# Gated delta mixer: a group's blocks are made and stored with its projections, and only their inversion stays in the next iteration

## The chip, the cores and the metric

The kernel runs on one core of one Trainium2 chip. The metric is the device time of one execution in microseconds (us); lower is better. Engine names: PE is TensorE, DVE is VectorE, ACT is ScalarE, POOL is GpSimd, SP is SyncE, which only issues DMAs here. Each engine works through its own instructions in the order in which they stand in the program.

## The reference

The program is a four-layer encoder trunk on 256 tokens of width 1024; each layer has a token mixer and a SwiGLU channel mixer. The change touches the mixer of layer 1, a bidirectional gated delta rule. It has 8 query and key heads, each serving 2 value heads of width 128. One direction of it, cut to what matters:

```python
decay = _exp_segsum(g_cs)                       # exp(g_i - g_j) for j <= i, else 0
a_mat = jnp.where(strict, jnp.einsum('bnhid,bnhjd->bnhij', k_beta, k) * decay, 0.0)
rhs = jnp.concatenate([v_beta, k_beta * jnp.exp(g_cs)[..., None]], axis=-1)
sol = lax.linalg.triangular_solve(a_mat, rhs, left_side=True, lower=True, unit_diagonal=True)
qk = jnp.einsum('bnhid,bnhjd->bnhij', q, k) * decay
...
o = rms_norm(o_fwd + o_bwd, norm_w) * jax.nn.silu(z.astype(f32).reshape(bt, L, GDN_V_HEADS, GDN_HEAD_DIM))
```

So for each head and direction a unit triangular matrix, made of key products and decays, has to be inverted or solved with.

## The kernel before, in words

The mixer (`gdn`, L554 to L842) works on 8 groups, one per query and key head; a group is 2 value heads, in two directions. The 256 tokens are taken as two blocks of 128. Four generators make the stages of a group `a`:

- `into(a)` (L609): projections of query and key (`pqk`) and of value (`pv`) on PE, a convolution and SiLU on DVE and ACT, norms, the masked products `km` of key with key (`kk`) and of query with key (`qkm`), and the values turned to token order (`vtok`).
- `base(a)` (L660): for each of the 2 heads `decay_exps` (L396): two matmuls into the PSUM bank `bc`, four ACT ops (L408) and one Exp (L409) give the decays `e`; POOL makes `off` (L669), DVE four diagonal blocks `u` (L672), POOL `e` times `qkm` (L676). POOL then stores the 8 blocks `u` to HBM (`gat`, L681) and loads the 64 inner blocks of 16 by 16 (`yr`, L688). ACT copies them (L689, L690), 28 POOL ops in 14 steps invert all 64 (L696, L698), ACT copies them back (L702, L703), and they go through HBM (`inv`, L705) to `dg` (L707).
- `levels(a)` (L710): POOL spreads `dg` and `u` (`lx` L717, `lb` L721), PE projects `z` (`pz`), and three rounds of small matmuls (`pst`, `pw`, `px`) with copies between them build the inverses of the 128 by 128 blocks (`ls`: L746, L771).
- `apply(a)` (L775): matmuls `pu` and `po`, a norm (`ysq` on ACT, `oms` on DVE, `omr` on POOL L820, `yo` on DVE), transposes `yt`, gating, the split `yh`, `yl`, and the output projection's first half (`first`, into `acc_o`). `yh` and `yl` of groups 0 to 6 also go to HBM (`spill`, L833). The second half of the output projection (`second`, PSUM `proj`) comes in the last three iterations and loads them back (`again`, L598: `ych`, `ycl`).

Iteration `a` of the loop at L839 weaves `apply(a-3)`, `levels(a-2)`, `base(a-1)` and `into(a)`, and from a = 8 on `second`. This is only the order in which the program is written. A scheduler of the tile framework then places the instructions of each engine by its own model of time and by the free buffers, and that order is fixed on the chip. PSUM has one bank `base`, shared by `bc` and `pz`, and one bank `side`, shared by `ss`, `pk` and `vp`. The buffers that the change bears on are `km` (4, also used by `ych` and `ycl`), `off` (7), `e` (8) and `u` (3).

Of the kernel before, what the change touches and what calls it, by code (L numbers as in the profile page):

```python
# [7 lines left out]
F32 = mybir.dt.float32  # L8
F32R = mybir.dt.float32r
# [3 lines left out]
P = 128  # L13
L = 256
# [28 lines left out]
class Trunk:  # L43
# [510 lines left out]
    def gdn(self, i):  # L554
        nc, t, j = self.nc, self.t, 0
        wk = self.mx
# [37 lines left out]
        st = {}  # L594
# [3 lines left out]
        def again(a):  # L598
            if a == 7:
                return ys[a]  # L600
            y = [wk.tile([P, 2, L], F32R, name=n, tag="km", bufs=4) for n in ("ych", "ycl")]
            for c in range(2):
                nc.sync.dma_start(y[c].bitcast(F32), spill[a, c])
            return y
# [4 lines left out]
        def into(a):  # L609
            pq = self.project(t["gdn_w"][a, 0], name="pqk")  # L610
            yield
            qk = wk.tile([P, 2, L], F32, name="qk", tag="qk", bufs=1)
            for m in range(2):
                self.conv_silu(pq, m, cw[:, a, m], qk[:, m])
                yield
            sq = wk.tile([P, 2, L], F32, name="qsq", tag="qsq", bufs=1)
            nc.scalar.square(sq, qk)
            pv = self.project(t["gdn_w"][a, 1], name="pv")
            yield

            ss = side[0].tile([P, 2, 2], F32, name="ss", tag=side[1])
            for m in range(2):
                for s in range(2):
                    nc.tensor.matmul(ss[:, m, s:s + 1], sq[:, m, s * P:(s + 1) * P], self.ones[:, 0:1], start=True, stop=True)
            qe, ke, kr, kn = (wk.tile([P, 2], F32, name=n, tag=n, bufs=b) for n, b in (("qe", 5), ("ke", 2), ("kr", 2), ("kn", 2)))
            nc.vector.tensor_scalar(out=ke, in0=ss[:, 1], scalar1=EPS, scalar2=None, op0=ALU.add)
            nc.vector.tensor_scalar(out=qe, in0=ss[:, 0], scalar1=EPS, scalar2=EPS * P, op0=ALU.add, op1=ALU.mult)
            nc.gpsimd.tensor_tensor(out=kn, in0=ke, in1=self.half.to_broadcast([P, 2]), op=ALU.pow)
            nc.vector.reciprocal(out=kr, in_=ke)
            nk = wk.tile([P, 2, 2, 2], F32, name="nk", tag="nk", bufs=5)  # L630
            nc.vector.tensor_tensor(out=nk, in0=nb.rearrange("p s (d h) -> p s d h", d=2)[:, :, :, 2 * a:2 * a + 2],
                                    in1=kr.unsqueeze(2).unsqueeze(3).to_broadcast([P, 2, 2, 2]), op=ALU.mult)
            yield
            vt = wk.tile([P, 2, L], F32, name="vt", tag="vt", bufs=1)
            for m in range(2):
                self.conv_silu(pv, m, cw[:, a, 2 + m], vt[:, m])
                yield
            pair = []
            for m, mask in ((1, strict), (0, self.incl)):
                pk = side[0].tile([P, 2, L], F32, name="pk", tag=side[1])  # L640
                for s in range(2):
                    nc.tensor.matmul(pk[:, s], qk[:, 1, s * P:(s + 1) * P], qk[:, m], start=True, stop=True)
                km = wk.tile([P, 768], F32, name="km", tag="km", bufs=4)
                self.masked(km, pk, mask)
                pair.append(km)
                yield
            kk, qkm = pair
            vs = []
            for m in range(2):
                vp = side[0].tile([P, 2, P], F32, name="vp", tag=side[1])  # L650
                for s in range(2):
                    nc.tensor.transpose(vp[:, s], vt[:, m, s * P:(s + 1) * P], self.ident)
                v = wk.tile([P, 2, P], F32, name="vtok", tag="vtok", bufs=8)
                for s in range(2):
                    nc.scalar.activation(v[:, s], vp[:, s], AF.Copy, scale=kn[:, s:s + 1])
                vs.append(v)
                yield
            st[a] = kk, qkm, vs, nk, qe

        def base(a):  # L660
            kk, qkm, vs, nk, qe = st[a]
            u = wk.tile([P, 8, P], F32, name="u", tag="u", bufs=3)
            es, offs = [], []
            for m in range(2):
                h = 2 * a + m
                e = self.decay_exps(pos, row, h, 32 + h, 8, bank)
                yield
                off = wk.tile([P, 2, P], F32, name="off", tag="off", bufs=7)
                nc.gpsimd.tensor_tensor(out=off.rearrange("p a b -> p (a b)"), in0=e[:, 128:384], in1=kk[:, 128:384],  # L669
                                        op=ALU.mult)  # L670
                for o, s, d in blocks:
                    nc.vector.scalar_tensor_tensor(out=u[:, 4 * d + 2 * m + s], in0=e[:, o:o + P],  # L672
                                                   scalar=nk[:, s, d, m:m + 1], in1=kk[:, o:o + P],
                                                   op0=ALU.mult, op1=ALU.mult)
                yield
                nc.gpsimd.tensor_tensor(out=e, in0=e, in1=qkm, op=ALU.mult)  # L676
                es.append(e)
                offs.append(off)
                yield
            gat = self.dr.tile([64, 2064], F32, name=f"gat{a}")  # L680
            nc.gpsimd.dma_start(gat.rearrange("(u b) x -> u (b x)", b=8)[:, :P * P].rearrange("u (p c) -> p u c", c=P), u)  # L681
            yield

            yb = lambda n: wk.tile([64, 16, 16], F32, name=n, tag=n, bufs=1)
            yr, y = yb("yr"), yb("yb")
            fl = lambda v, p: v[p].rearrange("p r c -> p (r c)")
            fw, bw = slice(0, 32), slice(32, 64)
            nc.gpsimd.dma_start(yr, gat[:, :16 * P].rearrange("q (r c) -> q r c", c=P)[:, :, :16])  # L688
            nc.scalar.copy(fl(y, fw), fl(yr, fw))  # L689
            nc.scalar.copy(fl(y, bw), fl(yr, bw)[:, ::-1])  # L690
            yield
            for k in range(1, 15):
                sh = [64, k, 15 - k]
                tm = wk.tile([64, 64], F32, name="ybt", tag="ybt", bufs=2)[:, :k * (15 - k)].rearrange(
                    "p (r c) -> p r c", r=k)
                nc.gpsimd.tensor_tensor(out=tm, in0=y[:, :k, k:k + 1].to_broadcast(sh),  # L696
                                        in1=y[:, k:k + 1, k + 1:].to_broadcast(sh), op=ALU.mult)
                nc.gpsimd.tensor_tensor(out=y[:, :k, k + 1:], in0=y[:, :k, k + 1:], in1=tm, op=ALU.add)  # L698
                yield
            nc.gpsimd.memset(y.rearrange("p r c -> p (r c)")[:, ::17], 1.0)  # L700
            yo = yb("yr")
            nc.scalar.copy(fl(yo, fw), fl(y, fw))  # L702
            nc.scalar.copy(fl(yo, bw), fl(y, bw)[:, ::-1])  # L703
            inv = self.dr.tile([8, 8, 16, 16], F32, name=f"inv{a}")
            nc.gpsimd.dma_start(inv.rearrange("u b r c -> (u b) r c"), yo)  # L705
            dg = wk.tile([P, 8, 16], F32, name="dg", tag="dg", bufs=2)
            nc.gpsimd.dma_start(dg, inv.rearrange("u b r c -> (b r) u c"))  # L707
            st[a] = es, vs, offs, u, dg, nk, qe
# [66 lines left out]
        def apply(a):  # L775
# [58 lines left out]
            if a > 0:  # L834
                first(a - 1)

        first, second, close = self.halves(t["gdn_wo"], ys.get, again)
        run = lambda f, a: [f(a)] if 0 <= a < 8 else []
        for a in range(11):  # L839
            weave(*run(apply, a - 3), *run(levels, a - 2), *run(base, a - 1), *run(into, a),  # L840
                  *([second(*((0, 1, 2), (3, 4), (5, 6))[a - 8])] if a > 7 else []))
# [530 lines left out]
```

## Time and profile before

| | |
|---|---|
| runs (3): median, lowest, highest | 2034.78 us, 2032.54 us, 2035.58 us |
| the profiled execution: its time, its span | 2029.43 us, 2027.7 us |
| mean granted TensorE clock | 0.932 |
| PE, DVE, ACT, POOL busy, share of the span | 88%, 71%, 52%, 17% |

The profile is of one execution, and its times are counted from the start of its span. The gated delta mixer lies at about 525 to 940 us. Its loop over the groups begins with the first `pqk`, and the last output projection of the mixer ends at about 938 us. A busy share is an average over stages with different limits; the prediction reads the stretch of this mixer alone. A row of the timeline has the start, the duration, the engine, the line, the operation with output and inputs, and in brackets the idle time of the engine before it and what ended that.

### The profile page before, as it was taken

How to read it: one execution, taken by the hardware profiler on the slowest of the kernel's cores; microseconds unless marked ns; L12 is line 12 of the kernel's file. 1: busy time of each engine (PE TensorE's matmuls, PEld its weight loads, DVE VectorE, ACT ScalarE, POOL GpSimd, SP SyncE). 2: the span in 40 equal slices, each digit the busy share in tenths (PEclk: the TensorE clock that was granted, in tenths of full speed). 3: DMA queues.
4: the chain of work that ended last, by engine and by line, in shares of the span. 5: the costliest groups of instructions: out<-in, count | busy, mean ns of one | idle time of the engine just before them, and what ended most of it. 6: DMA issues, size and time to landing. Idle time of an engine off the chain costs nothing.

```text
span 2027.7 us, 35637 instructions
## 1 busy us (share of the span) xinstructions
PE 1782.4 (88%) x13948; PEld 1526.6 (75%) x13948; DVE 1441.8 (71%) x2542; ACT 1044.9 (52%) x1888; POOL 353.7 (17%) x536
## 2 busy tenths in 40 slices
PE   5999969999599988975999976969997999978998
PEld 5899848888588877763878765658886899857886
DVE  5999957997788676434989458456646999946653
ACT  4777746553466556423545334444434677734442
POOL 1121110000167465621000002010001111110000
PEclk9999979999799999986999966979998999988999
DMA  6344335776344343612767587256644334416652
GB/s 230 118 134 146 115 105 163 243 223 210 120 138 133 99 122 101 182 46 102 236 201 238 175 302 194 68 198 186 187 152 163 125 130 141 127 52 202 185 185 93
DMA packets 105848, 317.66 MB, mean 157 GB/s; under 512 B 11036, under 2 KB 35180, under 8 KB 103632
## 3 DMA queue, kind: packets, MB, share of 16 engines
q1 hardware_dynamic: 99472, 296.03, 45.6%
q0 software_dynamic: 5920, 18.83, 3.1%
q8 instruction: 109, 1.79, 0.4%
q14 instruction: 59, 0.48, 0.1%
q10 hardware_dynamic: 288, 0.52, 0.1%
HBM read 287.49 MB, written 27.85 MB: 156 GB/s over the span
## 4 chain that ended last, share of the span: by engine, by line
PE 71%; DVE 11%; POOL 5%; ACT 5%; issue 4%; DMA 3%; SPq 0%; DVEq 0%; POOLq 0%; ACTq 0%
PE proj L87 10%; PE proj L88 10%; PE proj L89 10%; PE acc_o L87 5%; PE acc_o L88 5%; PE acc_o L89 5%; PE proj L94 5%; PE proj L95 4%; PE proj L96 4%; DVE wlo L80 3%; PE yp L525 2%; POOL ybt L696 2%; ACT whi L79 2%; POOL yb L698 1%; DMA s_w<-wt 1%
## 5 line engine op out<-in xcount | busy, mean ns | idle before, releaser
L80 DVE TENSOR_TENSOR wlo<-raw,whi 128x1024 fp32r<-128x1024 f32 x475 | 599.3, 1267 | 242.2 <-ACT whi L79 235.3
L79 ACT CAST whi<-raw 128x1024 fp32r<-128x1024 f32 x475 | 495.0, 1049 | 413.5 <-PE proj L88 180.8
L87 PE MATMUL proj<-whi,xh 128*128 128x512 f32 x768 | 307.7, 403 | 23.9 <-DVE xl L192 20.0
L89 PE MATMUL proj<-wlo,xh 128*128 128x512 f32 x768 | 304.2, 396 | 0.0
L88 PE MATMUL proj<-whi,xl 128*128 128x512 f32 x768 | 304.2, 396 | 0.0
L94 PE MATMUL proj<-xh,whi 128*128 128x256 f32 x792 | 232.7, 295 | 9.2 <-DVE acc L421 5.0
L96 PE MATMUL proj<-xh,wlo 128*128 128x256 f32 x792 | 229.4, 290 | 0.0
L95 PE MATMUL proj<-xl,whi 128*128 128x256 f32 x792 | 227.3, 287 | 0.0
L87 PEld LDWEIGHTS proj<-whi,xh 128*128 128x128 f32 x768 | 147.2, 192 | 57.5 <-DVE xl L192 21.6
L87 PE MATMUL acc_o<-whi,yh 128*128 128x512 f32 x448 | 179.6, 404 | 5.8 <-ACT yh L191 5.8
L218 POOL TENSOR_TENSOR rs<-ms,mhalf 128x1 f32<-128x1 f32 x32 | 20.9, 653 | 935.0 <-DVE ms L217 930.8
L88 PE MATMUL acc_o<-whi,yl 128*128 128x512 f32 x448 | 179.2, 400 | 0.0
L89 PE MATMUL acc_o<-wlo,yh 128*128 128x512 f32 x448 | 176.3, 396 | 0.0
L89 PEld LDWEIGHTS proj<-wlo,xh 128*128 128x128 f32 x768 | 146.8, 191 | 31.4 <-issue 0.2
L88 PEld LDWEIGHTS proj<-whi,xl 128*128 128x128 f32 x768 | 147.2, 192 | 30.9 <-issue 0.7
L94 PEld LDWEIGHTS proj<-xh,whi 128*128 128x128 f32 x792 | 155.0, 196 | 15.6 <-DVE acc L421 5.8
L95 PEld LDWEIGHTS proj<-xl,whi 128*128 128x128 f32 x792 | 155.3, 196 | 0.1
L96 PEld LDWEIGHTS proj<-xh,wlo 128*128 128x128 f32 x792 | 155.0, 196 | 0.3
L408 ACT ACTIVATE e<-bc,csn 128x256 f32<-128x256 f32 (+1 forms) x320 | 108.7, 430 | 39.0 <-PE bc L403 39.0
L255 PE MATMUL ht<-ident,xn 128*128 128x128 f32 x128 | 29.2, 381 | 108.8 <-DVE xn L287 48.1
L421 DVE SCALAR_TENSOR_TENSOR acc<-proj,cw,acc 128x255 f32<-128x255 f32 (+1 forms) x256 | 118.3, 476 | 2.0
L500 POOL TENSOR_TENSOR e<-e,cbm 128x768 f32<-128x768 f32 x32 | 60.7, 1897 | 324.1 <-DVE cbm L852 130.7
(357 smaller groups left out, 3416.8 us busy)
## 6 DMA issues: line engine op xcount, KB each, us to landing
raw<-w_gu SPq DMA_DIRECT2D x176, 512.0 KB, 4.5
raw<-ssd_w SPq DMA_DIRECT2D x96, 512.0 KB, 3.8
raw<-w_dn SPq DMA_DIRECT2D x88, 512.0 KB, 3.6
raw<-gdn_w SPq DMA_DIRECT2D x48, 512.0 KB, 4.2
raw<-ssd_wo SPq DMA_DIRECT2D x32, 512.0 KB, 3.5
nwb<-norm_w POOLq DMA_DIRECT2D x16, 512.0 KB, 5.1
s_w<-wt SPq DMA_DIRECT2D x16, 512.0 KB, 5.4
s_cl<-clb SPq DMA_DIRECT2D x16, 512.0 KB, 5.2
```

What stands on the lines that cost most here:

```text
L79: nc.scalar.copy(hi, raw)
L80: nc.vector.tensor_tensor(out=lo, in0=raw, in1=hi.bitcast(F32), op=ALU.subtract)
L87: nc.tensor.matmul(out, x[0], w[0], start=first, stop=False, **kw)
L88: nc.tensor.matmul(out, x[1], w[0], start=False, stop=False, **kw)
L89: nc.tensor.matmul(out, x[0], w[1], start=False, stop=last, **kw)
L94: nc.tensor.matmul(out, hi, x[0], start=first, stop=False, **kw)
L95: nc.tensor.matmul(out, hi, x[1], start=False, stop=False, **kw)
L96: nc.tensor.matmul(out, lo, x[0], start=False, stop=last, **kw)
L408: nc.scalar.activation(e[:, o], src, AF.Relu, scale=-1.0, bias=n)
L421: nc.vector.scalar_tensor_tensor(out=acc[:, a:b], in0=ps[:, m, a + o:b + o], scalar=cw[:, k:k + 1], in1=acc[:, a:b], op0=ALU.mult, op1=ALU ...
L500: (nc.gpsimd if hl % 2 == 0 else nc.vector).tensor_tensor(out=es[hl], in0=es[hl], in1=cbm, op=ALU.mult)
L525: nc.tensor.matmul(yp[64 * hh:64 * hh + 64, m, a:b], xdt[:, s, d, 2 * m + hh], es[2 * m + hh][:, o:o + b - a], start=(n == 0), stop=(n == 3))
```

## The change

The second half of `into(a)` now also makes the decays, `off`, `u`, `e` times `qkm` and the store `gat` of group `a`; `base(a)`, an iteration later, begins with the load `yr`. In iteration `a` these instructions are now written for group `a`, where they were for group `a-1`. `km` gets 3 buffers where it had 4, `off` 8 where it had 7. The number of instructions and their operands stay the same. Lines behind the edit move down by at most 3.

```diff
-            y = [wk.tile([P, 2, L], F32R, name=n, tag="km", bufs=4) for n in ("ych", "ycl")]
+            y = [wk.tile([P, 2, L], F32R, name=n, tag="km", bufs=3) for n in ("ych", "ycl")]
...
-                km = wk.tile([P, 768], F32, name="km", tag="km", bufs=4)
+                km = wk.tile([P, 768], F32, name="km", tag="km", bufs=3)
...
-            st[a] = kk, qkm, vs, nk, qe
-
-        def base(a):
-            kk, qkm, vs, nk, qe = st[a]
+
             u = wk.tile([P, 8, P], F32, name="u", tag="u", bufs=3)
             es, offs = [], []
             for m in range(2):
                 h = 2 * a + m
                 e = self.decay_exps(pos, row, h, 32 + h, 8, bank)
                 yield
-                off = wk.tile([P, 2, P], F32, name="off", tag="off", bufs=7)
+                off = wk.tile([P, 2, P], F32, name="off", tag="off", bufs=8)
                 nc.gpsimd.tensor_tensor(out=off.rearrange("p a b -> p (a b)"), in0=e[:, 128:384], in1=kk[:, 128:384],
                                         op=ALU.mult)
...
             nc.gpsimd.dma_start(gat.rearrange("(u b) x -> u (b x)", b=8)[:, :P * P].rearrange("u (p c) -> p u c", c=P), u)
-            yield
+            st[a] = es, vs, offs, u, nk, qe, gat
+
+        def base(a):
+            es, vs, offs, u, nk, qe, gat = st[a]
 
             yb = lambda n: wk.tile([64, 16, 16], F32, name=n, tag=n, bufs=1)
```

How the scheduler's order moves is shown at three places; numbers behind a tile's name are those of its buffer.

**POOL, around the store of group 6.** Before; ahead of these rows stand the 28 ops of group 5's inversion and `omr` of `apply(3)`, and `off_9826` and `e_9722` belong to group 7:

```order
L707 DMA dg_9045<-inv5_9043 128x8x16
L833 DMA spill_5411<-yh_8772 128x512
L717 TENSOR_TENSOR lx_9060<-dg_9045,lev_5319 128x256
L833 DMA spill_5411<-yl_8773 128x512
L669 TENSOR_TENSOR off_9484<-e_9347,km_8941 128x256
L676 TENSOR_TENSOR e_9347<-e_9347,km_8962 128x768
L681 DMA gat6_9553<-u_9067 128x8x128
L721 TENSOR_TENSOR lb_9712<-u_9067,lev_5319 32x256 x4
L669 TENSOR_TENSOR off_9826<-e_9722,km_9592 128x256
L688 DMA yr_9584<-gat6_9553 64x16x16
L676 TENSOR_TENSOR e_9722<-e_9722,km_9613 128x768
```

Now; ahead stand the 28 ops of group 5's inversion with `omr` of `apply(2)` among them:

```order
L833 DMA spill_5411<-yl_8145 128x512
L717 TENSOR_TENSOR lx_9095<-dg_9071,lev_5319 128x256
L628 TENSOR_TENSOR kn_9518<-ke_9516,half_69 128x2
L666 TENSOR_TENSOR off_9043<-e_9034,km_8962 128x256
L673 TENSOR_TENSOR e_9034<-e_9034,km_8983 128x768
L666 TENSOR_TENSOR off_9073<-e_9059,km_8962 128x256
L673 TENSOR_TENSOR e_9059<-e_9059,km_8983 128x768
L678 DMA gat6_9080<-u_9030 128x8x128
L721 TENSOR_TENSOR lb_9747<-u_9030,lev_5319 32x256 x4
L688 DMA yr_9102<-gat6_9080 64x16x16
```

Both products of both heads of a group now stand ahead of its store, where before the first head's stood behind the store of the group before. Counted against `apply`, the store is one group ahead: before, group 5's inversion stands next to `omr` of `apply(3)`, now group 6's does. `omr` itself stands behind 28, 20, 28, 28 and 20 of the 28 inversion ops for `apply(0)` to `apply(4)` before, and behind 7, 18, 17, 16 and 17 now.

**PE, the `bc` matmuls of group 1**, between the value projection of group 1 (`pv`) and `pz` of group 0; `vp` are transposes of group 0's values. Before:

```order
L96 MATMUL pv_5731<-xh_72,wlo_5728 128x256
L403 MATMUL bc_5910<-csr_5402,sel_82 128x256 x2
L652 MATMUL vp_5601<-ident_63,vt_5570 128x128 x2
L94 MATMUL pz_5992<-xh_72,whi_5982 128x256
L95 MATMUL pz_5992<-xl_73,whi_5982 128x256
L96 MATMUL pz_5992<-xh_72,wlo_5983 128x256
```

Now:

```order
L96 MATMUL pv_5754<-xh_72,wlo_5751 128x256
L403 MATMUL bc_5886<-csr_5402,sel_82 128x256 x2
L652 MATMUL vp_5601<-ident_63,vt_5570 128x128 x2
L403 MATMUL bc_5911<-csr_5402,sel_82 128x256 x2
L652 MATMUL vp_5607<-ident_63,vt_5570 128x128 x2
L94 MATMUL pz_6022<-xh_72,whi_6012 128x256
```

The second head's `bc`, which stood an iteration later and amid a projection, now follows the first with one pair of transposes between them, and `pz`, in the same PSUM bank, follows with another pair. Group 2 has its two `bc` pairs likewise; from group 3 on a projection or other work lies between the two.

**SP, the loads of the tail.** `ych` and `ycl` of groups 0 to 2, between weight loads (`raw`). Before:

```order
L603 DMA ych_9736<-spill_5411 128x512
L603 DMA ycl_9737<-spill_5411 128x512
L603 DMA ych_9838<-spill_5411 128x512
L603 DMA ycl_9839<-spill_5411 128x512
L76 DMA raw_10273<-gdn_w 128x1024
L76 DMA raw_10279<-gdn_w 128x1024
L76 DMA raw_10334<-gdn_wo 128x1024
L603 DMA ych_9912<-spill_5411 128x512
L603 DMA ycl_9913<-spill_5411 128x512
```

Now:

```order
L603 DMA ycl_9767<-spill_5411 128x512
L603 DMA ych_9865<-spill_5411 128x512
L603 DMA ycl_9866<-spill_5411 128x512
L603 DMA ych_9941<-spill_5411 128x512
L76 DMA raw_10273<-gdn_w 128x1024
L76 DMA raw_10279<-gdn_w 128x1024
L76 DMA raw_10334<-gdn_wo 128x1024
L603 DMA ycl_9942<-spill_5411 128x512
L603 DMA ych_10244<-spill_5411 128x512
```

Before, a group's two loads stand together; `ych_9736` is group 0's. Now group 0's `ych` stands four rows earlier, and group 2's `ycl` (`ycl_9942`) stands behind three weight loads. With 3 buffers a group's `ycl` takes the buffer that the `ych` of the group before had.

## Rows read from the trace of the kernel before

**Rows 1.** Busy time by windows: PE, PEld, DVE, ACT, POOL, clock, DMA share, GB/s.

```profile
560.00:600.00 40.00, 35.01 (x258) 33.62 (x257) 37.32 (x73) 26.70 (x53) 28.62 (x46) 0.93 0.51 160
...
760.00:800.00 40.00, 34.03 (x541) 29.87 (x540) 28.07 (x56) 22.46 (x54) 25.10 (x45) 0.94 0.31 98
```

**Rows 2.** The chain that ended last, 676 to 880 us, by line.

```profile
by line: POOL ybt L696 11.2%; POOL yb L698 9.7%; issue 9.1%; DMA yr<-gat 6.2%; POOL lb L721 5.6%; ACT whi L79 3.5%; PE acc_o L87 3.5%; ACT e L408 3.2%; PE acc_o L88 2.7%; POOL e L676 2.2%; POOL omr L820 2.0%; PE acc_o L89 1.9%; PE px L768 1
```

**Rows 3.** Waits of PE, 560 to 840 us: total, times, longest.

```profile
PE pst L756 <- DVE ls L746: 4.8, 2, 3.9
PE yt L827 <- DVE yo L822: 4.5, 3, 1.9
PE pst L756 <- ACT ls L771: 3.3, 3, 2.4
PE pz L94 <- ACT e L408: 3.0, 3, 1.2
```

**Rows 4.** Timeline of PE, three places early in the loop.

```profile
551.19 0.79 PE L403 MATMUL bc<-csr,sel 128*128 128x256 f32 x2 [2.38 <-ACT e L408]
...
594.02 0.59 PE L652 MATMUL vp<-ident,vt 128*128 128x128 f32 x2 [2.36 <-DVE km L852]
595.61 0.58 PE L94 MATMUL pz<-xh,whi 128*128 128x256 f32 x1 [1.00 <-ACT e L408]
```

**Rows 5.** Timeline of ACT in the tail.

```profile
858.46 0.40 ACT L689 COPY yb<-yr 32x256 f32<-32x256 f32 x1 [2.76 <-DMA yr<-gat]
...
859.30 1.04 ACT L79 CAST whi<-raw 128x1024 fp32r<-128x1024 f32 x1
...
869.59 0.40 ACT L702 COPY yr<-yb 32x256 f32<-32x256 f32 x1 [5.04 <-POOL yb L698]
...
870.43 0.60 ACT L815 ACTIVATE ysq<-po 128x512 f32<-128x512 f32 x1
870.93 0.26 ACT L764 COPY sw<-pw 128x128 f32<-128x128 f32 x1
```

**Rows 6.** Timeline of DVE in the tail.

```profile
855.73 1.23 DVE L80 TENSOR_TENSOR wlo<-raw,whi 128x1024 fp32r<-128x1024 f32 x1 [1.16 <-ACT whi L79]
860.38 1.23 DVE L80 TENSOR_TENSOR wlo<-raw,whi 128x1024 fp32r<-128x1024 f32 x1 [3.42 <-ACT whi L79]
...
861.78 1.70 DVE L746 TENSOR_TENSOR ls<-lx,px 32x256 f32<-32x256 f32 x4
```

**Rows 7.** Timeline of PE in the tail.

```profile
831.70 0.65 PE L827 MATMUL yt<-ident,yo 128*128 128x128 f32 x4 [1.92 <-DVE yo L822]
...
858.75 0.69 PE L744 MATMUL px<-lx,lw 32*32 32x32 f32 x56
863.63 0.61 PE L756 MATMUL pst<-ident,ls 32*32 32x32 f32 x32 [4.19 <-DVE ls L746]
...
868.47 0.47 PE L762 MATMUL pw<-sT,u 32*32 32x32 f32 x32
871.24 0.47 PE L768 MATMUL px<-ls,sw 32*32 32x32 f32 x32 [2.30 <-ACT sw L764]
```

**Rows 8.** DMA issues: KB each, median us from issue to landing.

```profile
ycl<-spill SPq DMA_DIRECT2D x7, 256.0 KB, 2.9
```

**Rows 9.** Waits of POOL, 560 to 945 us.

```profile
POOL off L669 <- ACT e L409: 23.8, 5, 8.1
```

**Rows 10.** Timeline of POOL: the second head of group 5, its store, the first product of group 6.

```profile
769.34 0.74 POOL L669 TENSOR_TENSOR off<-e,km 128x256 f32<-128x256 f32 x1 [8.07 <-ACT e L409]
...
779.52 0.86 POOL L688 DMA_DIRECT2D yr<-gat  x1
780.39 1.82 POOL L676 TENSOR_TENSOR e<-e,km 128x768 f32<-128x768 f32 x1
```

**Rows 11.** Instructions on tile u: duration in ns, min/median/max, first and last start.

```profile
L672 DVE SCALAR_TENSOR_TENSOR u<-e,nk,km x64: 339/351/1322, 564.7 to 846.3; 128x128 f32<-128x128 f32 x64
```

**Rows 12.** Instructions on tile ybt, in the same form.

```profile
L696 POOL TENSOR_TENSOR ybt<-yb x112: 205/270/1357, 580.4 to 869.1; 64x14 f32<-64x14 f32 x16, 64x26 f32<-64x26 f32 x16, 64x36 f32<-64x36 f32 x16, 64x44 f32<-64x44 f32 x16
```

## The prediction, as it was made before the run

> **What bounds the kernel now.** The change touches one mixer, so I read that mixer's stretch and not the page's shares of the whole span. First the busy time by windows [rows 1]: in the middle of the loop over the groups PE is busy for 34.03 of 40 us, and no other engine for more than 28.07. At its start DVE is the fullest, with 37.32 of 40. So the loop is bound by PE with some idle time, except at its start, where an idle PE is partly the shadow of a full DVE. Next the chain that ended last [rows 2]: from 676 to 880 us it lies for 37% (11.2, 9.7, 6.2, 5.6, 2.2 and 2.0) on the inversion's POOL ops, the load `yr`, `lb`, `e` and `omr`. So POOL is tied into the chain although PE has the work. What that costs PE is in PE's waits [rows 3]: 4.8 us for `ls` from DVE, 4.5 for `yo`, which waits for `omr`, 3.3 for `ls` from ACT, 3.0 for the decays that hold the bank of `pz`. These 15.6 us are most of what a better order inside the loop can win. The tail's waits [rows 7] are read below. The chain alone would promise far more than the waits allow: while the chain runs through POOL, PE mostly has other work.
>
> **The change, part by part.** Nothing is removed or added. Per group these move one iteration earlier: two `bc` pairs on PE, two times five ops on ACT, eight `u` on DVE, two `off` and two `e` products and one store on POOL. Their sum is the same, so only places and buffers can change the time. Outside this mixer every engine's order stays the same.
>
> 1. **The tail, a gain.** Before, the inversion of group 7 runs at 858 to 870 us, when few groups are left, and its ACT copies stand in ACT's queue ahead of things PE needs. Now that inversion lies one group earlier and these copies stand before the last projection's work. First place: ACT waits 2.76 us for `yr` [rows 5], the weight conversion behind it begins only at 859.30, DVE's subtraction at 860.38 and the four `ls` adds at 861.78 [rows 6], and PE waits 4.19 us [rows 7]. Without the copies the subtraction follows the one that ended at 856.96, and the adds can start when `px` ends at 859.44; they take 1.70, so PE goes on at about 861.3 in place of 863.63: 2.3 us. Second place: ACT waits 5.04 us for the inversion's end [rows 5], with `ysq` and `sw` behind it, and PE's `px` waits 2.30 [rows 7]. `po` is through at 868.47; `sw` comes 0.5 behind `ysq` and `px` 0.3 behind `sw`, so 869.3 in place of 871.24: 1.9 us. Together **-4.2**. What is late next there is the chain `ysq`, `oms`, `omr`, `yo`, `yt`, which moves up with them.
>
> 2. **The loads of the tail, a loss.** With 3 buffers, a group's `ycl` can be loaded only when the group before it has left PE; a load takes 2.9 us to land [rows 8]. Groups 1 and 2, and 2 and 3, stand close together on PE. Between 1 and 2 only short `px` work and two matmuls lie, some 1.2 us, so 1.7 us are open; but PE already idles 1.92 us there for `yt` [rows 7], and that wait falls into the same gap, which leaves 0.5. Between 2 and 3 `yt` (0.65) and some 1 us of small matmuls lie: 1.2 open. SP's queue holds the next weights behind a waiting load, but they are for later groups. Taken: **+1.7**. Bounds: 0, and 5.8 if both loads are fully bare.
>
> 3. **The two `bc` pairs side by side, a loss at the start.** The second needs the first's bank. At 551.19 such a second pair waited 2.38 us [rows 4]; one pair of transposes (0.59) now lies between, which leaves 1.8, for groups 1 and 2, and `pz` of group 0 waits 1.8 in place of about 1.0 [rows 3]: 4.4 in all. DVE is 93% busy there [rows 1], so I take half: **+2.2** (bounds 0 and 4.4). From group 3 on a projection covers the first head's decays; without that cover each group would pay 2.4.
>
> 4. **Waits that go at the start.** `vp` of group 1 waited 2.36 us for `km` through the bank `side`, and `pz` 1.00 [rows 4]; in the new order a value projection lies ahead of that `vp`, and `pz` comes earlier. 3.4, and half for the same reason: **-1.7** (bounds 0 and -3.4).
>
> 5. **`omr` earlier in POOL's queue.** It stands behind 16 to 18 inversion ops instead of 20 or 28. PE's three waits for `yo` inside the loop's full part sum to 4.5 us [rows 3], the tail's 1.92 is in term 2. Where it stood behind all 28, the wait should go (1.1); where behind 20, three ops of some 0.3 us [rows 12] go. Taken: **-1.8** (bounds 0 and -4.5).
>
> 6. **DVE's order near `ls`.** In DVE's new order the adds of `levels(4)` stand ahead of a weight subtraction (1.23 [rows 6]) and one SiLU product instead of behind them, but behind two mask products more. PE waited up to 3.9 us for them [rows 3]. Taken: **-1.0** (bounds 0 and -3.9).
>
> 7. **The store later on POOL.** Both heads' decays and the first `e` product now stand ahead of the store; before, the next group's first product (1.82) ran in the shadow of the `yr` load [rows 10]. POOL waited 23.8 us in five times for decays ahead of `off` [rows 9], 4.8 a time, and I take it that this slack covers the 1.82: **0**. If it does not, 1.82 for each of groups 3 to 7: 9.1.
>
> 8. **The rings.** `e` now has all 8 buffers in flight. The decays of group a+4 wait for `po` of group a, and PE's order has that `po` ahead of the `bc`: nothing. `u` keeps 3 and is free when `levels` of three groups back has ended, just ahead of the new `bc`: nothing.
>
> Sum: -4.2 + 1.7 + 2.2 - 1.7 - 1.8 - 1.0 = **-4.8 us**. The profiled execution took 2029.43, so its like would take 2024.6. The median of the runs is 2034.78, 5.35 above that execution; on its scale the forecast is **2030.0 us**. What a measurement here can tell from no change is about 0.2%, 4.1 us; the forecast lies just beyond that.
>
> **A rule against it.** Of 64 `u` products of one shape half take under 351 ns and the longest 1322 [rows 11]; the small POOL products run from 205 to 1357 [rows 12]. The Trainium skill, page "SBUF — State Buffer", section "Who interferes with whom", says that a DVE instruction with two SBUF inputs and a POOL instruction that reads SBUF take turns: the first has the shared ports for its whole length. By that rule, with which these spreads agree, the second head's `u` now meet the first head's `e` product ahead of every store.
>
> **The rivals.**
>
> *Slower: the store sets the pace.* Each store now waits for a second head's decays (about 2.4 us, the wait at 551.19 [rows 4]) and an `e` product (1.82). The slack is 4.8 a time [rows 9]; a `u` product held up once costs a further 1.0 (1322 less 351 ns [rows 11]), which makes 5.2 and is more than the slack. So this decides from the point where the decays come that late. Against it: the 8.07 us wait [rows 10]. Price: 9.1 for five groups, and the 1.8 of term 5 is lost because the inversion starts later: -4.8 + 9.1 + 1.8 = +6.1, 2040.9 us; with a held-up `u` in each of the five, 2045.8.
>
> *No change: the loads eat the tail's gain.* Both loads bare (5.8 for 1.7): -0.7, 2034.1 us. For it: SP's strict queue. Against it: the `yt` gap.
>
> *A larger gain: the slots follow the chain.* If the 37% of the chain [rows 2] is a true cycle (store, load, inversion, `omr`, `yt`, next decays), the group ahead breaks it, and PE's 15.6 us of waits [rows 3] go: -15.6 - 4.2 + 1.7 = -18.1, 2016.7 us. Against it: PE's waits change hands when an order is new, and seldom all go.
>
> *The scheduler keeps the old places.* The order shows the inversion one group ahead from group 3 on, so there is little for it: 2034.8.
>
> **How the numbers follow.** Forecast 0.43, slower rival 0.24, no change 0.18, larger gain 0.12, old places 0.03. The forecast lies near the border, and its unknown terms spread it by several us: of its 0.43 I count 0.34 as faster and 0.09 as within 0.2%. Faster: 0.34 + 0.12 = 0.46. Same: 0.09 + 0.17 + 0.03 = 0.29. Slower: 0.24, and 0.01 of the no-change case: 0.25. The range takes in all of the forecast's bounds, the slower rival nearly to its end and most of the larger gain: 2018 to 2045.
>
> **What would show it.** Right: the wait of 4.19 at the last but one `levels` falls to about 2 and ACT has no `yr` copy between 850 and 880 us of the old scale; `omr` follows `oms` within 1 us; two new waits of PE for decays appear near 570 and 595 us; PE waits for `ycl` once or twice near 830 us. Wrong: `off` on POOL no longer waits for decays but for POOL itself, PE's waits for `yo` grow, and the first output matmuls of successive groups (`acc_o`) come further apart than before. Then term 7 was not free.

## The result, and the profile after

The changed kernel takes 2048.05 us (median of 4 runs), the kernel before 2034.03 us beside it: a ratio of 1.0069, 95% interval 1.0052 to 1.0087. It is **slower by 14 us**, where the prediction had it faster by 4.8. The profiled execution after has a span of 2047.7 us.

First the whole stretch, from the first decay matmul to the first matmul behind the mixer's last sum: PE's busy time, then PEld, DVE, ACT, POOL, the granted clock, the DMA share. Before:

```profile
548.00:939.50 391.50, 336.64 (x4545) 299.12 (x4545) 243.61 (x490) 198.29 (x443) 205.81 (x367) 0.92 0.35 107
```

After:

```profile
550.70:957.80 407.10, 345.60 (x4544) 305.79 (x4544) 247.14 (x490) 199.09 (x443) 213.97 (x367) 0.89 0.33 102
```

The stretch is 15.6 us longer. The two profiled executions differ by more than the medians do (spans of 2027.7 and 2047.7 us, 20.0 apart against 14.0), since that of the kernel before was a short one; the other 4.4 us lie outside the stretch. The same matmuls keep PE busy for 9.0 us more, with a granted clock of 0.89 in place of 0.92, and PE is idle for 6.6 us more (61.5 against 54.9). More than half of these 15.6 us is thus PE working more slowly, and no term of the prediction has that.

Where it happens: I gave every PE instruction a weight (the lower fifth of the spacing of its kind over the profiles), summed from the first decays, and looked how much later than in the kernel before the same sum is reached. This **lag** is a working figure from one execution each, and lags of a few us say nothing by themselves: a kernel that is level in time with the kernel before (e8 below) has 3.6 at 921 us. After the change it is 6.1 us at 576 us of the old scale, 13.8 at 639, and from there it stays between 10 and 21, with 17.1 at 921. So the loss is made while the loop fills, in two steps, and is not won back. The windows of the two steps, before:

```profile
568.00:578.00 10.00, 8.37 (x69) 7.96 (x68) 9.61 (x19) 8.21 (x19) 8.70 (x8) 1.00 0.60 165
578.00:588.00 10.00, 10.00 (x83) 9.89 (x82) 8.72 (x17) 7.76 (x15) 6.66 (x17) 1.00 0.51 166
588.00:598.00 10.00, 6.64 (x41) 5.97 (x40) 10.00 (x22) 6.18 (x13) 8.90 (x18) 0.81 0.53 176
598.00:608.00 10.00, 10.00 (x75) 10.00 (x75) 7.72 (x15) 4.58 (x10) 6.23 (x9) 0.85 0.26 86
```

And after, 3 us later on the scale:

```profile
571.00:581.00 10.00, 5.59 (x29) 4.75 (x28) 8.61 (x19) 9.06 (x23) 8.45 (x7) 0.78 0.60 166
581.00:591.00 10.00, 10.00 (x74) 9.90 (x74) 4.00 (x11) 3.70 (x7) 7.20 (x21) 0.88 0.02 3
591.00:601.00 10.00, 9.59 (x78) 9.29 (x76) 9.96 (x19) 4.70 (x8) 9.16 (x16) 1.00 0.60 193
601.00:611.00 10.00, 4.20 (x18) 3.67 (x19) 9.11 (x14) 8.21 (x22) 6.81 (x6) 0.64 0.53 180
```

PE begins 199 matmuls in these 40 us where it began 268. DVE and ACT are not fuller but emptier (31.7 against 36.0 us, 25.7 against 26.7): nobody is overloaded, everybody waits for somebody. What PE waits for, in PE's timeline after; the brackets hold the idle time before a row:

```profile
571.23 0.39 PE L403 MATMUL bc<-csr,sel 128*128 128x256 f32 x2
572.53 0.41 PE L652 MATMUL vp<-ident,vt 128*128 128x128 f32 x2 [0.91 <-DVE km L852]
573.67 0.50 PE L403 MATMUL bc<-csr,sel 128*128 128x256 f32 x2 [0.73 <-ACT e L408]
575.40 0.44 PE L652 MATMUL vp<-ident,vt 128*128 128x128 f32 x2 [1.23 <-ACT vtok L655]
577.38 0.58 PE L94 MATMUL pz<-xh,whi 128*128 128x256 f32 x1 [1.54 <-ACT e L408]
...
605.78 0.80 PE L403 MATMUL bc<-csr,sel 128*128 128x256 f32 x2 [4.17 <-ACT e L408]
608.03 0.58 PE L94 MATMUL pqk<-xh,whi 128*128 128x256 f32 x1 [1.45 <-DVE acc L421]
```

At the first step PE thus idles 4.4 us in four waits. Before, the same place had two, of 1.6 us together:

```profile
569.73 0.41 PE L652 MATMUL vp<-ident,vt 128*128 128x128 f32 x2 [0.90 <-DVE km L852]
570.87 0.39 PE L94 MATMUL pz<-xh,whi 128*128 128x256 f32 x1 [0.73 <-ACT e L408]
```

The two waits that are new are 1.54 us of `pz` for the bank `base` and 1.23 us of the second transposes for `vtok`, which empties the bank `side`.

And before, the second pair of group 1 came one projection later, at no wait at all:

```profile
584.31 0.28 PE L403 MATMUL bc<-csr,sel 128*128 128x256 f32 x1
585.10 0.47 PE L403 MATMUL bc<-csr,sel 128*128 128x256 f32 x1
```

At the second step the decays themselves are late. ACT works in order, and ahead of them stand two weight casts that wait for their loads:

```profile
599.55 1.05 ACT L79 CAST whi<-raw 128x1024 fp32r<-128x1024 f32 x1 [3.60 <-DMA raw<-gdn_w]
...
602.97 1.05 ACT L79 CAST whi<-raw 128x1024 fp32r<-128x1024 f32 x1 [1.09 <-DMA raw<-gdn_w]
...
604.38 1.35 ACT L408 ACTIVATE e<-bc,csn 128x256 f32<-128x256 f32 x4
```

The first pair's matmul ended at 600.6 and was read from 604.38 on. That ACT keeps its order is also in the Trainium skill, page "PSUM — Partial Sum Buffer", section "Engine vs sequencer instructions": the queues of ScalarE, VectorE and GpSimd are strict FIFO. The trace agrees: the decays were read 3.8 us after their matmul, behind the casts, and PE's next pair waited 4.17 us. DMA had stood nearly still (share 0.02) at 581 to 591. I take that to be why the loads are late: PE had left `pz` after 18 of its 48 matmuls for `pqk`, so that the weights of both stayed in use.

What did the earlier decays buy there? The store of group 1, before and after:

```profile
592.37 0.96 POOL L681 DMA_DIRECT2D gat<-u  x1 [0.24 <-issue]
```

```profile
595.41 0.96 POOL L678 DMA_DIRECT2D gat<-u  x1
```

That is 44.4 and 44.7 us behind the first decays: nothing. Before, the scheduler had already put group 1's decays early enough for that store, one pair beside each projection.

PE's waits after, 560 to 850 us, the lines that answer to [rows 3] and the new ones:

```profile
PE pst L756 <- ACT ls L771: 6.1, 2, 4.9
PE bc L403 <- ACT e L408: 5.4, 3, 4.2
PE vp L652 <- DVE km L852: 4.8, 4, 2.1
PE proj L88 <- DMA ycl<-spill: 2.4, 1, 2.4
PE pz L94 <- ACT e L408: 2.0, 2, 1.5
PE yt L827 <- DVE yo L822: 1.9, 2, 1.0
```

The tail, which answers to [rows 7]:

```profile
838.06 0.51 PE L88 MATMUL proj<-whi,ycl 128*128 128x512 f32 x1 [2.38 <-DMA ycl<-spill]
...
885.86 0.47 PE L756 MATMUL pst<-ident,ls 32*32 32x32 f32 x32 [2.60 <-DVE ls L746]
...
891.67 0.47 PE L768 MATMUL px<-ls,sw 32*32 32x32 f32 x32 [0.44 <-ACT sw L764]
```

### The profile page after: what moved, and what is told of

It is laid out like the page before. It is cut to its first block, busy times and chain, and to the rows that moved or that the text cites. A ratio compares the mean times of both kernels' runs of the same rounds, so it can differ in the third digit from the quotient of the medians.

```text
span 2047.7 us, 35626 instructions
## 1 busy us (share of the span) xinstructions
PE 1794.5 (88%) x13948; PEld 1536.6 (75%) x13948; DVE 1445.7 (71%) x2542; ACT 1048.6 (51%) x1888; POOL 361.3 (18%) x536
## 4 chain that ended last, share of the span: by engine, by line
PE 68%; DVE 13%; DMA 5%; POOL 5%; ACT 4%; issue 4%; SPq 0%; DVEq 0%; POOLq 0%; ACTq 0%
PE proj L87 10%; PE proj L88 9%; PE proj L89 9%; PE acc_o L87 5%; PE acc_o L88 5%; PE acc_o L89 4%; PE proj L94 4%; PE proj L95 4%; PE proj L96 4%; DVE wlo L80 3%; PE yp L525 2%; DVE acc L421 1%; ACT whi L79 1%; POOL ybt L696 1%; POOL yb L698 1%
## 5 line engine op out<-in xcount | busy, mean ns | idle before, releaser
L88 PEld LDWEIGHTS proj<-whi,xl 128*128 128x128 f32 x768 | 148.0, 193 | 31.3 <-issue 0.7
L94 PEld LDWEIGHTS proj<-xh,whi 128*128 128x128 f32 x792 | 155.5, 197 | 15.6 <-DVE acc L421 5.8
```

Source lines behind the costliest of these rows:

```text
L88: nc.tensor.matmul(out, x[1], w[0], start=False, stop=False, **kw)
L94: nc.tensor.matmul(out, hi, x[0], start=first, stop=False, **kw)
```

## The experiments

All times are ratios to the kernel before, run beside each kernel, with the 95% interval; the lag is at 576, 639 and 921 us of the old scale. The execution that gives a lag is not always a typical one: executions of e10 spread over 12 us and its profiled one is the longest (2046.70 us, median 2038.76), as are those of e9 and e15; those of e1 and e14 are the shortest (2037.81 and 2040.95 us, medians 2044.95 and 2046.21).

| kernel | ratio | lag, us |
|---|---|---|
| the change | 1.0069 (1.0052 to 1.0087) | 6.1, 13.8, 17.1 |
| e1 groups 0 to 3 moved | 1.0046 (1.0031 to 1.0061) | 6.1, 13.7, 10.9 |
| e2 groups 4 to 7 moved | 1.0002 (0.9987 to 1.0017) | 2.1, 1.1, 1.2 |
| e11 groups 3 to 7 moved | 1.0005 (0.9990 to 1.0020) | 0.1, 3.4, -3.2 |
| e8 buffers alone | 1.0004 (0.9991 to 1.0017) | 0.4, 0.7, 3.6 |
| e3 change, `km` 4 | 1.0093 (1.0077 to 1.0110) | 5.2, 12.3, 21.0 |
| e14 decays alone moved | 1.0058 (1.0043 to 1.0073) | 5.3, 11.8, 8.1 |
| e9 change, second bank | 1.0123 (1.0104 to 1.0143) | 5.2, 10.5, 31.3 |
| e5 change, `pz` first | 1.0088 (1.0065 to 1.0112) | 5.8, 13.3, 13.7 |
| e10 change, decays apart | 1.0028 (1.0013 to 1.0044) | 0.9, 10.8, 10.2 |
| e15 e10 with `pz` first | 1.0076 (1.0055 to 1.0098) | 1.5, 16.5, 15.1 |
| e4 change, copies on POOL | 1.0001 (0.9984 to 1.0017) | 6.2, 11.3, 4.8 |
| e7 e4 with `pz` first | 1.0015 (1.0000 to 1.0029) | 6.1, 13.3, 3.3 |
| e13 e10, copies on POOL | 1.0003 (0.9990 to 1.0016) | 1.3, 13.3, 0.3 |
| e16 e15, copies on POOL | 0.9990 (0.9977 to 1.0003) | 1.6, 6.5, 1.7 |
| e6 before, copies on POOL | **0.9958** (0.9942 to 0.9974) | 2.2, 3.7, -11.3 |
| e12 e6, group 7 moved | 0.9969 (0.9955 to 0.9983) | 0.4, 3.2, -4.8 |
| e17 e6, groups 3 to 7 moved | **0.9950** (0.9936 to 0.9963) | 0.6, 4.1, -9.3 |

**Which groups.** The moved lines became a generator `made(a)`, called from `into` or from `base`:

```diff
+        MOVED = (0, 1, 2, 3)
...
+            if a in MOVED:
+                yield from made(a)
...
         def base(a):
+            if a not in MOVED:
+                yield from made(a)
+                yield
```

> The blocks of groups 0 to 3 alone are made and stored with their projections; groups 4 to 7 are as before, and km keeps 4 buffers (off 8). Early theory (the loss arises where the loop fills: two pairs of decay matmuls side by side, and ACT's in-order queue held up by the inversion's copies that wait for the load yr or for POOL's loop): the trace after is 12 us behind at the first output matmul of group 0 and 18 behind at that of group 2, so this kernel keeps most of it and lacks the gain of the tail: +12 to +20 us over the kernel before, 2046 to 2054. Buffer theory (km with 3 buffers, above all the late loads of the tail): nothing is left of the loss, within 3 us of the kernel before. Store theory (each moved group's store is about 1.8 us later on POOL, from group 3 on): one store of five, +1 to +3.

> The other half: only the blocks of groups 4 to 7 are made and stored with their projections; groups 0 to 3 are as before, km keeps 4 buffers (off 8). Early theory: the filling of the loop is as before, the wait of 4.19 us in the tail goes, so -2 to -6 us against the kernel before, 2028 to 2032, if the held-up copies cost nothing in the full part. Store theory: four later stores of five at 1.8 us less the tail's gain of about 4, so +2 to +6. Buffer theory: with 4 buffers no late loads, so -2 to -6 too.

> The blocks of groups 3 to 7 made and stored with their projections, groups 0 to 2 as before; km 4 buffers, off 8. From group 3 on a projection stands beside the decays. If the loss is the filling of the loop (either theory of it): no steps at 571 and 600, -4 to +3 us against the kernel before, 2030 to 2037. Store theory (five later stores at 1.8): +4 to +8.

The first half alone has both steps to the tenth, and +0.46%; the second half and groups 3 to 7 cost nothing that can be measured. So most of the loss is made in the filling of the loop. The five later stores of e11 cost nothing either, and the store theory falls. e1 was expected at +12 to +20 us and came to 9.4: in its profiled execution 3 us of the lag are won back behind the groups that are as before. The tail's gain did not show as time in e2: its lag rises to 10 in the full part and falls to 1 in the tail.

**Buffers.**

```diff
-name="off", tag="off", bufs=7)
+name="off", tag="off", bufs=8)
...
-tag="km", bufs=4)
+tag="km", bufs=3)
```

> The kernel before with the changed numbers of buffers alone (km 3, off 8) and no move. Buffer theory: +5 to +14 us, 2039 to 2048. Early theory: up to the late loads of the tail, -1 to +4 us, 2033 to 2038.

> The changed kernel with km at 4 buffers in place of 3, nothing else. The order of PE up to the tail is word for word that of the changed kernel. Buffer theory: PE's waits for the loads ych and ycl, 6.8 us after against 2.2 before, fall back, and with them up to 4.6 us of the 14; if the buffers were the whole cause, all 14. Early theory: at most those 4.6, so 2043 to 2049, and the first output matmul of group 3 still stands about 16 us later than before. Store theory: no change beyond the 4.6 either.

e8 is that edit in the kernel before, and nothing changes. e3 gives the changed kernel its fourth `km` back: PE's waits for `ycl` behind 785 us fall from 5.9 to 1.2 and it is slower still, above every range that was expected for it (1.0093). In its tail PE has other waits (8.3 for `yo` where 4.0 were); that they are the reason is not shown. The buffers are not the cause of the loss, and waits for loads are not yet time.

**The decays alone.**

```diff
+            ee = []
+            for m in range(2):
+                ee.append(self.decay_exps(pos, row, 2 * a + m, 32 + 2 * a + m, 8, bank))
+                yield
...
-                e = self.decay_exps(pos, row, h, 32 + h, 8, bank)
-                yield
+                e = ee[m]
```

The first lines stand in `into`, the last in `base`, with everything else of the kernel before.

> The kernel before (km 4, off 7) with the decays alone (the matmuls into bc and their five ACT ops a head) made with the projections, as the changed kernel has them; the products off, u and e, the store and the load stay where they were. PE's order at the start is that of the changed kernel, the two pairs side by side and pz and pqk interleaved. In-order theory: the place of the decays makes the loss, so both steps appear, and +9 to +15 us, 2043 to 2049. Load theory with the products on DVE and POOL as the load, and store theory: no or little loss, -3 to +4, 2031 to 2038.

Both steps are there, and +0.58%. So it is the place of two matmuls and five ACT ops a head that makes most of the loss. The products and the store that moved along are not shown to be free: e3, which also has four `km` buffers and moves everything, is at 1.0093, clear of 1.0058, and what makes that rest is open.

**The first step.** Two ways to part the pairs:

```diff
-                e = self.decay_exps(pos, row, h, 32 + h, 8, bank)
+                e = self.decay_exps(pos, row, h, 32 + h, 8, (bank, side)[m])
```

> The changed kernel with the second head's decay matmuls in the PSUM bank side in place of base, so that they need not wait until ACT has emptied the first head's bank. Measured by the PE work done, the changed kernel falls 6 us behind at the decays of group 1 (571 to 581) and another 6 to 9 at those of group 2 (600 to 611), and keeps that lag to the end. Bank theory (each of these two steps comes from two pairs of decays that follow each other through one bank, and from the clock that PE loses in the pause): both steps go, 9 to 13 us are won back, 2035 to 2039. Load theory (at the start ACT and DVE have no time for a further group's decays and blocks, whichever bank they stand in): the steps stay, within 3 us of the changed kernel, 2045 to 2051.

Both theories missed. With `side` the scheduler put the second head of group 0 behind the transposes of that bank, and later PE met a new wait of 7.73 us for the decays. The first step stayed (5.2 us) though the pairs stand in two banks: there the transposes and one pair of decays follow each other through `side`, with four waits of 3.8 us in all at 573 to 579. In e10 the decays are called behind `pqk` and behind `pv` in place of the end of `into`:

> The changed kernel with the decays written earlier in into: the first head's behind pqk, the second's behind pv; the products stay where they are. In PE's order the two pairs of group 1 now have the whole value projection between them, while those of group 2 still follow each other (a transpose between them). Bank theory: the first step of 6 us goes and the second stays, 2041 to 2044. Load theory: ACT has the same ops ahead of the convolutions, so both steps stay or grow, 2046 to 2053.

As the bank theory said, the first step goes and the second stays: the pairs of group 1 stand at 564.51 and 572.21 with `pv` between, the first step falls from 6.1 to 0.9 us, and the time from 1.0069 to 1.0028. But `pz` now also stands between the two pairs of transposes, so that both new waits of the first step are gone. With e9 this points to short matmuls in a row, without a projection between, as what makes the first step; that the bank `base` alone makes it is not shown. The windows of e10, PE's clock at 1.00 where it was 0.78 and 0.88:

```profile
571.00:581.00 10.00, 7.45 (x59) 6.93 (x57) 9.56 (x20) 7.52 (x19) 9.30 (x8) 1.00 0.54 160
581.00:591.00 10.00, 10.00 (x80) 9.79 (x79) 6.92 (x20) 6.37 (x10) 6.14 (x15) 1.00 0.22 61
```

**The second step.** In e5 `pz` of group 0 is written ahead of `pqk` of group 2:

```diff
         def into(a):
+            for _ in range(1 if a == 2 else 0):
+                yield
```

> The changed kernel, with one more yield at the head of into(2), so that pz of group 0 is written ahead of pqk of group 2. In the changed kernel PE starts pz, leaves it after 18 of 48 matmuls for pqk, and comes back 8 us later, so the weights of two projections are in use at once; here PE's order has pz in one piece. Start theory (the second pair of decays delays pz, the two projections interleave, the weight loads stall, their casts hold ACT's queue, the decays of group 2 come late): DMA is busy again between the two projections (share 0.02 there after, 0.51 before), the wait of 4.17 us for the decays falls to 2.4 or less, and with the clock that the idle PE lost 5 to 9 us come back, so 2039 to 2043. If only the bank between the two pairs counts: the wait stays near 4, no more than 2 us are won, 2046 to 2049. If only the copies on ACT count: 2046 to 2049 too.

The loads came earlier (share 0.20 in place of 0.02), no cast waited for one, and no wait for decays was over 2.5 us, yet the step stayed and the time did not fall. In e10 something else held the decays, with ACT's row and then PE's:

```profile
607.68 0.40 ACT L705 COPY yr<-yb 32x256 f32<-32x256 f32 x1 [7.08 <-POOL yb L701]
...
608.52 1.36 ACT L408 ACTIVATE e<-bc,csn 128x256 f32<-128x256 f32 x4
```

```profile
609.93 0.58 PE L94 MATMUL pz<-xh,whi 128*128 128x256 f32 x1 [11.74 <-ACT e L408]
```

The copy of the inverse waits for POOL's loop, and the decays wait behind the copy. So e4 puts the four copies on POOL, which waits for the same things anyway:

```diff
-            nc.scalar.copy(fl(y, fw), fl(yr, fw))
+            nc.gpsimd.tensor_copy(fl(y, fw), fl(yr, fw))
```

and the same in the three other copies.

> The changed kernel with the four copies around the inversion (yr to y, y to yo) on POOL in place of ACT, for all groups, so that no ACT instruction waits for the load yr or for POOL's loop. Early theory, its part on ACT's queue: PE's waits for ACT's ls (6.1 us), for sT (1.7), and part of those for the decays and km go, 8 to 14 us in all, so 2034 to 2040 in place of 2048; POOL's loop gets longer by four small copies a group, which costs nothing as long as the next stage's weights are not waiting for it. Start theory alone (the two pairs side by side and late weights): no more than 3 us are won. Store theory: POOL is the bound, and 32 copies of some 0.4 us more on it make the time longer, 2050 to 2060.

All 14 us come back, as expected, and alone this would have passed for the proof that the copies are the cause. But the lag at the start is nearly the same as in the changed kernel. Hence the control, the same edit in the kernel before:

> Control: the four copies around the inversion on POOL in the kernel before, not the changed one. If the copies cost much only where the change puts them: the tail's wait of 4.19 us goes and little else, -2 to -5 us against the kernel before, 2029 to 2032. If they hold ACT up as much wherever they stand: -8 to -13, 2021 to 2026, and then the move itself is not to blame for what e4 won back. If POOL is short of time: 0 to +5.

It gains 0.42%. The copies cost both kernels, so they explain a part of the difference at most: with them on POOL the move still costs 0.43% (1.0001 against 0.9958), with them on ACT 0.69%, and the intervals are too wide to tell these two costs apart. The views of e6 show what went. ACT's waits for the copies' inputs, before, 548 to 940 us:

```profile
ACT yr L702 <- POOL yb L698: 18.5, 7, 5.0
...
ACT yb L689 <- DMA yr<-gat: 10.1, 5, 2.8
```

are gone, and PE's waits for `ls` fell from the first line (before) to the second (e6, 551 to 931 us):

```profile
PE pst L756 <- DVE ls L746: 11.0, 4, 4.2
```

```profile
PE pst L756 <- DVE ls L746: 2.2, 2, 2.0
```

The scheduler moved other things too, so the 0.42% is that of the edit, not of these waits alone. Then the combinations:

> The changed kernel with both: pz of group 0 ahead of pqk of group 2, and the copies around the inversion on POOL. If the start and the copies are two separate causes, the gains add: 12 to 13 from the copies (e4) and 5 to 9 from the start, 2026 to 2031, faster than the kernel before. If they are one cause (late ACT work at the start), no more than e4 alone: 2033 to 2037.

> The changed kernel with the decays written apart (as e10) and the copies around the inversion on POOL (as e4). In e10 the first step was gone, and at the second the decays of group 2 stood in ACT's queue behind the copy L702, which waited 7.08 us for POOL's loop, so that PE waited 11.74 us. In-order theory (both steps are decays that come late, the first through the bank, the second through what stands ahead of them in ACT's queue): neither step is left, the lag in PE's work at 620 is under 4 us, and the time is that of e6 or better with the tail's gain, 2018 to 2028. Load theory (ACT and DVE have too much to do at the start): the second step stays at some 9 us, 2032 to 2038.

> As e10 (the decays written apart in into), and pz of group 0 written ahead of pqk of group 2 (as e5). In e10 the bank base was held from 575 to 592 by pz, which PE had left for pqk, so that both pairs of group 2 came after the value projection; here PE's order has pz in one piece, the first pair of group 2 ahead of its value projection and the second behind it. Bank theory (each step is two pairs of decays that follow each other through base without a projection between): neither step is left, the lag at 620 falls from 12 us to 4 or less, and the time to that of the kernel before or below it by the tail's gain, 2029 to 2036. If the second step has another cause (the inversion of group 0, which POOL and ACT share with the blocks of group 1): it stays at 6 to 9 us, 2038 to 2043.

> As e15, with the copies around the inversion on POOL. e13, the same without pz ahead, was at 1.0003 and kept a second step of 12 us, at which PE waited 7.35 us for lx from POOL. Bank theory: the step goes, 0.994 to 0.997, 2022 to 2028, about as e6 or below it. If the second step has another cause: 1.000 again, 2032 to 2037.

e7 is no faster than e4 (1.0015 and 1.0001), so the gains do not add. e15 came out above both of its ranges (1.0076). e13 and e15 keep the second step, each with another wait in front; these two rows are of e13 and e15:

```profile
615.62 1.08 PE L735 MATMUL pst<-ident,lx 32*32 32x32 f32 x64 [7.35 <-POOL lx L720]
```

```profile
615.83 1.44 PE L629 MATMUL ss<-ones,qsq 128*128 128x1 f32 x6 [4.01 <-ACT qsq L622]
```

e16, with pairs apart, `pz` first and the copies off ACT, has less than half of it (4.9 us where e13 has 12.0), and there PE waits 4.69 us for `lx`. So parting the pairs takes the first step away, and not the second. **Open:** what alone makes the second. Casts, copies and POOL's loop stand one behind the other there, and each edit that took one wait away left another.

**A version that beats both.**

> The best of both: the copies around the inversion on POOL, and only group 7's blocks made and stored with its projections (km 4, off 8). e6 without any move is at 0.9958 of the kernel before. If the tail's gain of about 4 us by the earlier inversion comes on top: 0.993 to 0.9955, 2020 to 2025. If the copies on POOL have won the same waits already: within 0.1% of e6, 2023 to 2027.

> The blocks of groups 3 to 7 alone moved (as e11) and the copies around the inversion on POOL (as e6). e11 had no step at the start and ended level with the kernel before; e6 was at 0.9958. If the move from group 3 on costs and gains nothing beside the copies: 0.995 to 0.997, 2024 to 2028. If its earlier inversions help once ACT's queue is free: below 0.995, under 2024. If they bring POOL, which now also copies, into PE's way in the full part: 0.998 to 1.001, 2030 to 2036.

e12 is no faster than e6, so the tail's gain does not come on top. e17, the move without the filling of the loop and with the copies on POOL, is at 0.9950 (2025.07 us beside 2035.75), e6 without any move at 0.9958. Their intervals overlap: the gain is that of the copies, and the move in the full part and the tail is worth nothing that these runs can tell.

## Why the prediction was wrong

It failed at **term 3**, the two `bc` pairs side by side at the start. I saw the place and a part of the mechanism, and took +2.2 us, half of a bound of 4.4, because DVE was 93% busy there; with the -1.7 of term 4 the start was to cost 0.5. In its place the runs showed a lag of 13.8 us by 639 us, and e14, with the decays alone moved, is 0.58% slower, 11.8 us. Three things were wrong in the term.

- *The bound was no bound.* I priced only waits for the bank `base`. Those of `bc` at 548 to 660 us rose from 2.4 to 7.3 us, and those of `pz` fell from 1.7 to 1.5: 4.7 more, just above the bound, with 4.17 at group 2, where I had 1.8. ACT's queue makes that one longer: the decays stand behind casts that wait for their loads. The transposes' 1.23 us for `vtok` had no term.
- *The discount was wrong.* The waits came in full. A full DVE in the kernel before was no cover: in the new order it is less busy there too (4.00 of 10 us at 581 to 591).
- *The clock had no term.* Each pause was followed by a stretch at a lower granted clock (0.78 and 0.88 at the first step, 0.64 at the second, a mean between the levels of 1.2 and 2.4 GHz). Over the stretch PE is busy 9.0 us more, of 15.6. The last section has runs in which this share is smaller.

The rest, term by term:

- **Term 1 (tail, -4.2): right in the waits.** 4.19 became 2.60 and 2.30 became 0.44, 3.5 us less. It is not shown that this shortened the run.
- **Term 2 (loads, +1.7): too small as a wait, of no account as time.** PE's waits for `ych` and `ycl` rose from 2.2 to 6.8 us, but e8, with 3 buffers, has 5.4 us of them at no cost, and e3 is slower without most of them.
- **Term 4 (waits that go at the start, -1.7): wrong.** `vp` waited 3.3 us for `km` before, now 1.8 for `km` and 1.8 for `vtok`; `pz` 1.7, now 1.5. The waits changed hands.
- **Term 5 (`omr`, -1.8): wrong in the mechanism.** `omr` did not come sooner: for groups 1 to 3 it starts 3.1, 2.9 and 2.5 us behind `oms`, before 2.8, 1.7 and 0.8, because inversion ops still stand ahead of it. The 4.5 us of waits for `yo` also hold the tail's 1.92, which I had put into term 2; the other two, 1.45 and 1.10, became 1.00 and 0.91, 0.6 us less.
- **Term 6 (DVE's order, -1.0): near in the sum.** The waits for DVE's `ls` went (4.8 us), those for ACT's grew from 3.3 to 6.1.
- **Term 7 (the store, 0): right.** POOL's waits for decays fell from 23.8 [rows 9] to 8.7 us, and e2 and e11 show no cost of the later stores.
- **Term 8 (rings, 0): right as far as ACT's waits show**, which have none of `e` for `po`.

The slower rival was right in its sign and wrong in its mechanism: its 2040.9 to 2045.8 us came from the store, and e11 has five later stores at no loss while e14 has the loss without them. With the store goes the weight that I gave to the Trainium skill's page "SBUF — State Buffer", section "Who interferes with whom": the products on DVE and POOL that I put its rule on do not move in e14, so their taking of turns is not what made most of the loss. Of the marks that I had set, three of the right ones came true (the tail's waits, the two new waits for decays, the waits for `ycl`), one failed (`omr` within 1 us of `oms`), and of the wrong ones one came true (the first output matmuls of groups 0 to 2 come 9, 16 and 18 us later, counted from the first decays). Each mark fitted a term, and none asked how much PE had done by then.

## What to carry to other kernels

Before you move work one iteration earlier, look whether the scheduler already does it where the loop fills: there the earlier place gained 0 us for the store and lost the projection between two pairs of decays. Small ops in one engine's queue that wait for another engine's loop can be worth moving to that engine: here four small copies, moved from ACT to the POOL that they waited for, gave 0.4%. And run the control: an edit that wins the loss back in the changed kernel (e4) proves nothing until it has been tried in the kernel before (e6).

## What the runs showed of the hardware

New pauses of PE can cost more through its granted clock than by themselves: after the change 6.6 us more idle time in the stretch came with 9.0 us more busy time for the same matmuls. But there is no fixed rate. In e5, which has both steps too, PE is idle 13.7 us more than before and not busy for longer:

```profile
551.70:956.80 405.10, 336.58 (x4544) 299.24 (x4545) 243.66 (x490) 199.54 (x443) 205.87 (x367) 0.91 0.33 103
```

And in e1, whose lag at the start is that of the change, PE is idle 7.8 us more and busy 1.0 us more.

The copies of 32x256 that take 404 ns on ACT (median) took 568 ns on POOL in e6, between 387 and 1062.
